# Interleaving the projection blocks of a two-layer encoder group by group, and taking weight scaling, rotation products and norm chains off two engines

## The chip, the cores and the metric

The kernel runs on one core of a Trainium2 chip. A core has five engines with queues of their own: TensorE (PE in the profile, with its weight loads as PEld), VectorE (DVE), ScalarE (ACT), GpSimd (POOL) and SyncE (SP), which issues the DMA transfers here. The metric is the device time of one execution in microseconds (us). Before the change it was 2788.43 us, the median of 3 runs (2785.87 to 2791.42).

## What is computed

The input x has 2048 positions of 1024 channels. Each of two layers computes

```python
h = rmsnorm(x, pre_g[l])
proj = jnp.einsum('bsd,de->bse', h, w_in[l])
u_a, v_a, g_a, q, k, v, g_b = jnp.split(proj, idx, axis=-1)
y_a = gmlp_group(u_a, v_a, ln_a_g[l], ln_a_b[l], spatial_w[l], spatial_b[l]) * jax.nn.silu(g_a)
y_b = gqa_axial_attention(q, k, v, q_norm_g[l], k_norm_g[l], tables) * jax.nn.silu(g_b)
y = jnp.concatenate([y_a, y_b], axis=-1)
x = x + rmsnorm(jnp.einsum('bse,ed->bsd', y, w_out[l]), post_g[l])
```

The projection has 2816 columns: u, v and g of the gating part (512 each), q (512: 8 heads of 64), k and v (128 each) and g_b (512). Gating layer-normalises v, mixes it over positions inside chunks of 128 (`W_s v + b`) and multiplies it by u and silu(g). Attention has 8 query heads on 2 key heads, with a root-mean-square norm and an axial rotation on every q and k head.

## The kernel before, in words

**Precision.** A product is made in three passes. Each operand is split into a high part and a low part, and high x high, high x low and low x high are summed in PSUM (`PASSES`). So a block of 256 columns for 128 positions takes 3 x 8 = 24 products.

**Two phases a layer.** `Project.run` makes the projection, `attend` the attention and the output product. The change touches the first. Positions are worked on in 4 groups of 512, each of 4 tiles of 128. `hT_jobs` loads a tile of x (L330), squares it on ACT for the norm (L334), computes the reciprocal root with 8 one-column operations on DVE (`rsqrt_row_steps`, L135 to L139), scales the tile on DVE (L339), transposes it on PE, and leaves a high part (ACT, L349) and a low part (DVE, L350) in `hT`. In the second layer the tiles of groups 0 and 1 arrive already scaled from the end of the layer before. The x rows live in a pool of 5 buffers.

**Weights.** A block of 256 columns is loaded (L262). `split_w` multiplies it by the norm weight `g_col` in two halves on GpSimd (L277), takes the largest magnitude on DVE (L280), spreads it over partitions by a product (tile `pe`), derives a power of two, and writes the high part on ACT (L294) and the low part on DVE (L295), each in two halves of 1024 elements.

**Blocks of a layer, in PE's order before.** (1) For each group: the k and v block, then q block 0; (2) q block 1 for all groups; (3) the v block of gating for all groups, 48 products a tile; (4) g_b blocks 0 and 1, each for all groups; (5) four gate blocks of 128 g and 128 u columns, each for all groups, 48 products of 512 columns. What follows a block on the other engines differs widely. A q block goes through `norm_rope`: squares on ACT (L390) and sums on DVE (L391), a reciprocal root in 10 operations (L123 to L127), the scaling (L398), the product with the cosines on GpSimd (L400), four products with the sines on DVE (L403) and the sum (L405), for two banks; later a transposition and a low part (L451). A k block does the same at half the width, plus L436. A g_b block takes one tanh on ACT and one DVE operation a bank (L515, L516). The rotation table is loaded per group and multiplied by the gain on GpSimd (L382).

**Background jobs.** `Background` holds small jobs with due times in ticks. `proj_tok` ticks once every 8 products of 256 columns, `proj_ch` once every 4 products of 512, and a tick runs up to two due jobs. Transpositions of the next group, second halves of `split_w` (`rest`), the mixing of v (L488) and the row maxima of the scores for the first 8 attention units (`max_step`: one product of 512 columns into `pmax` and one reduction on DVE, L748, per tick, 128 of them a layer) run this way. `last_jobs` enters the maxima; before the change it is called between steps (3) and (4).

**What fixes the order.** PE's order is that of the program (`Pinned`). The queues of DVE, ACT, GpSimd and SP are ordered by a scheduler when the kernel is built; each engine then works its queue strictly in that order. PSUM has 7 banks for all these tiles.

Of the kernel before, what the change touches and what calls it, by code (L numbers as in the profile page):

```python
# [9 lines left out]
F32 = mybir.dt.float32  # L10
F32R = mybir.dt.float32r
# [28 lines left out]
def encoder(ctx: ExitStack, tc, x, w_in, w_out, pre_g, post_g, ln_a_g, ln_a_b,  # L40
# [100 lines left out]

    def rsqrt(ms, n, tag):
        y, steps = rsqrt_steps(ms, n, tag, nc.vector)
        for f in steps:
            f()
        return y
# [30 lines left out]
    class Project:  # L177
# [88 lines left out]
        def split_w(self, raw, delay, vec=False):  # L266
# [3 lines left out]
            col = small.tile([P, 16], F32, name="w_col", bufs=5)  # L270
            top, sq, inv = col[:, 0:2], col[:, 2:4], col[:, 4:5]
            w.e, w.u, w.hu, w.hu2, w.eps = [col[:, 8 + i:9 + i] for i in range(5)]
            for i in range(2):
                sl = slice(i * ND // 2, (i + 1) * ND // 2)
                engine = nc.vector if vec and i == 0 else nc.gpsimd
                g = self.g_col[:, sl].unsqueeze(2).broadcast_to([P, ND // 2, WB])
                engine.tensor_tensor(raw[:, sl], raw[:, sl], g, ALU.mult)  # L277
            for i in range(2):
                sl = slice(i * ND // 2, (i + 1) * ND // 2)
                nc.vector.tensor_reduce(top[:, i:i + 1], raw[:, sl].rearrange("p d e -> p (d e)"), AX.X, ALU.max,  # L280
                                        apply_absolute_value=True)
            nc.vector.tensor_tensor(sq, top, top, ALU.mult)

            def rest():
                ps = ps_t("pe")
                for i in range(2):
                    PE.matmul(ps[:, 0:1], spread_w, sq[:, i:i + 1], start=(i == 0), stop=(i == 1))
# [4 lines left out]
                for i in range(2):  # L292
                    sl = slice(i * ND // 2, (i + 1) * ND // 2)
                    nc.scalar.activation(w.hl[:, 0, sl], raw[:, sl], AF.Copy, scale=w.e)  # L294
                    nc.vector.scalar_tensor_tensor(w.hl[:, 1, sl].rearrange("p d e -> p (d e)"),  # L295
                                                   raw[:, sl].rearrange("p d e -> p (d e)"), w.e,
                                                   w.hl[:, 0, sl].rearrange("p d e -> p (d e)"),
                                                   ALU.mult, ALU.subtract)
# [14 lines left out]
        def hT_jobs(self, g, tail=False):  # L313

            hT = big_t([P, 2, ND, GRP], "hT", F16)
            xs = [None] * TPG
            act, dve = (ACT, DVE) if tail else (nc.scalar, nc.vector)

            def prep(j):
                def f():  # L320
                    done = self.l > 0 and g < HN
                    src = h_d[g * TPG + j] if done else x_src(self.l, g * TPG + j)
                    if done:
                        xs[j] = xt = [f_t("x_h") for _ in range(2)]
                        for i in range(2):
                            nc.sync.dma_start(xt[i], src[:, i * GRP:(i + 1) * GRP])
                        return
                    row = row_t("x_t")
                    xs[j] = xt = [row[:, 0:GRP], row[:, GRP:D]]
                    nc.sync.dma_start(row, src)  # L330
                    junk = ps_t("sq")
                    parts = small.tile([P, 2], F32, name="ss_x", bufs=4)
                    for i in range(2):
                        nc.scalar.activation(junk, xt[i], AF.Square, accum_out=parts[:, i:i + 1])  # L334
                    z = small.tile([P, 1], F32, name="rs_x", bufs=4)
                    for f in rsqrt_row_steps(parts, z, "x", nc.vector):
                        f()
                    for i in range(2):
                        nc.vector.tensor_scalar(xt[i], xt[i], z, None, ALU.mult)  # L339
                return f  # L340
# [44 lines left out]
        def norm_rope(self, banks, n, tb, eps):  # L385
# [10 lines left out]
            for i, src in enumerate(banks):  # L396
# [3 lines left out]
                nc.gpsimd.tensor_tensor(t1, qn, tbi[:, :, 0:1, :].broadcast_to([P, 2, n, HD]), ALU.mult)  # L400
# [58 lines left out]
        def do_va(self, g, vs, ws):  # L459
# [8 lines left out]
            for j, vh in enumerate(vs):  # L468
# [9 lines left out]
                def mix(c, s=s, j=j):  # L478
# [12 lines left out]
                    if c == 3:  # L491
                        nc.sync.dma_start(z_d[g][:, :, j * P:(j + 1) * P], s.zt)
                bg.add(1 + 5 * j, split)
# [3 lines left out]
        def do_gate(self, g, c, pg, pu, w):  # L497
            z = f_t("fb")
# [65 lines left out]
        def run(self, kv, first, last_jobs, first_wo):  # L564
# [23 lines left out]
            w_kv = self.w_kv  # L588
            raw = self.load_w([C_Q])
            if self.l == 0:  # L590
                w = []
                bg.add(8, lambda: w.append(self.split_w(raw, None, True)))
            else:
                w = [self.split_w(raw, 6)]
            for i, g in enumerate(gs):
                if i == 0:
                    for f in self.stores:
                        f()
                    self.stores = []
                if i + 1 < NG:  # L600
                    start(g + 1)
                if i == 1:
                    raw = self.load_w([C_Q + WB])
                self.do_kv(g, self.banked(hTs[g], w_kv), w_kv)
                if i == 2:
                    w_next = self.split_w(raw, W_DELAY)
                    raw = self.load_w([C_VA])
                assert w and w[0].ready
                self.do_q(g, self.banked(hTs[g], w[0]), 0, w[0])
                if i + 1 < NG:  # L610
                    while left[g + 1]:
                        left[g + 1].pop(0)()
                if i == 1:
                    self.spatial_weights()
            w = w_next
            assert w.ready
            for i, g in enumerate(gs):
                if i == 0:
                    va = [self.split_w(raw, W_DELAY)]
                    raw = self.load_w([C_VA + WB])  # L620
                if i == 2:
                    va.append(self.split_w(raw, W_DELAY))
                    raw = self.load_w([C_GB])
                self.do_q(g, self.banked(hTs[g], w), 1, w)
            ws = [row_t("ws", dt=F32R) for _ in range(2)]
            for i in range(2):
                nc.sync.dma_start(ws[i].bitcast(F32), ws_d[:, i])
            assert va[1].ready
            for i, g in enumerate(gs):
                vs = []  # L630
                for j in range(TPG):
                    ps = self.proj_tok(hTs[g], j, va[0])
                    self.proj_tok(hTs[g], j, va[1], ps, WB)
                    v = f_t("fv")
                    for b in range(2):
                        sl = slice(b * WB, (b + 1) * WB)
                        nc.scalar.activation(v[:, sl], ps[:, sl], AF.Copy, scale=va[b].u)
                    vs.append(v)
                if i == 2:
                    w = self.split_w(raw, W_DELAY)  # L640
                    raw = self.load_w([C_GB + WB])
                self.do_va(g, vs, ws)
            nc.gpsimd.memset(self.kv[1][HD:HD + 2], 1.0)
            self.scale_v()
            last_jobs()
            blocks = [[C_GA + c * P, C_U + c * P] for c in range(4)]
            gbs = []
            for b in range(2):
                assert w.ready
                gbs.append(w)  # L650
                for i, g in enumerate(gs):
                    self.do_gb(g, self.banked(hTs[g], w), b, w)
                    if i == 1:
                        w_next = self.split_w(raw, W_DELAY)
                        raw = self.load_w(blocks.pop(0))
                w = w_next
            assert self.scaled
            for b in range(2):
                nc.vector.tensor_scalar(self.two_g[:, b], self.two, gbs[b].e, NORM_SCALE, ALU.mult, ALU.mult)
            for c in range(4):  # L660
                assert w.ready
                for i, g in enumerate(gs):
                    pg = self.proj_ch(hTs[g], w, 0)
                    pu = self.proj_ch(hTs[g], w, P)
                    self.do_gate(g, c, pg, pu, w)
                    if i == 1 and c < 3:
                        w_next = self.split_w(raw, W_DELAY)
                        raw = self.load_w(blocks.pop(0)) if blocks else None
                    if c == 3:
                        hTs[g] = None  # L670
                        if i == 1:
                            first_wo()
                w = w_next
# [620 lines left out]
```

## Time and profile before

| what | value |
|---|---|
| the profiled execution's own time | 2788.67 us |
| its span | 2786.9 us |
| median of 3 runs | 2788.43 us |
| PE busy | 2626.5 us (94% of the span) |
| DVE busy | 1891.0 us (68%) |
| ACT busy | 1500.0 us (54%) |
| POOL busy | 1361.8 us (49%) |
| first score product, layer 0 | 637.2 us from the span's start |
| first score product, layer 1 | 2015.3 us from the span's start |

The profile is of one execution. "Busy" is the time in which an engine had at least one instruction under way; PE's products are pipelined, so a busy PE need not be at its peak. The two projections take the stretches from the start to 637 us and from 1404 to 2015 us; attention takes the rest.

### The profile page before, as it was taken

What the parts mean: (1) busy time and instruction counts of PE and PEld (TensorE: products, weight loads), DVE (VectorE), ACT (ScalarE), POOL (GpSimd) and SP (SyncE); (2) the same over time, 40 slices, a digit from 0 to 9 for tenths busy, and PEclk for the clock granted to TensorE, in tenths of its full rate; (3) what the DMA queues carried; (4) which work ended last, traced back from release to release, by engine and by line L of the source; (5) the groups of instructions that cost most, each with busy time, mean ns of one, the idle gap of its engine ahead of it and who ended that gap; (6) DMA issues with size and microseconds to landing.
All of it is one profiled execution on the core that took longest, in us unless ns stands there. A gap on an engine that the chain in (4) does not pass through costs nothing. (4 is left out here: it accounts for less than half of the span.)

```text
span 2786.9 us, 48753 instructions
## 1 busy us (share of the span) xinstructions
PE 2626.5 (94%) x18318; PEld 1543.7 (55%) x18318; DVE 1891.0 (68%) x3978; ACT 1500.0 (54%) x3007; POOL 1361.8 (49%) x1121
## 2 busy tenths in 40 slices
PE   5788999999999999999978889999999999999997
PEld 4677976444444444444557778864444444444444
DVE  7978797435665766666498878983366656566664
ACT  3432211127887777877644222111288877777774
POOL 2233210116786776776642322001187767677764
PEclk9899999999999999999999999999999999999999
DMA  4232132332222222222533221323232212221313
GB/s 155 67 118 63 54 94 67 89 86 85 85 68 79 78 90 82 89 89 73 171 133 99 82 63 54 95 70 95 83 90 72 84 60 79 76 81 48 111 38 137
DMA packets 245329, 239.13 MB, mean 86 GB/s; under 512 B 20706, under 2 KB 204130, under 8 KB 245092
## 3 DMA queue, kind: packets, MB, share of 16 engines
q1 hardware_dynamic: 245092, 236.01, 27.4%
q8 instruction: 144, 2.36, 0.4%
q14 instruction: 93, 0.76, 0.1%
HBM read 150.88 MB, written 85.07 MB: 85 GB/s over the span
## 5 line engine op out<-in xcount | busy, mean ns | idle before, releaser
L84 POOL TENSOR_TENSOR p_parts<-p_f,p_parts 128x512 f16<-128x512 f32 x872 | 1033.3, 1204 | 395.4 <-ACT p_f L84 304.5
L84 ACT ACTIVATE p_parts<-sp 128x512 f16<-128x512 f32 x1024 | 627.0, 612 | 295.1 <-PE sp L84 288.0
L84 PE MATMUL pp<-w_hl,hT 128*128 128x256 f16 x5376 | 675.5, 279 | 9.9 <-DVE hT L350 5.8
L84 DVE TENSOR_REDUCE mx<-pmax 128x1 f32<-128x512 f32 x768 | 511.1, 680 | 233.4 <-PE pmax L84 231.2
L84 PE MATMUL pout<-wo,y_t 128*128 128x512 f32 x1488 | 655.4, 504 | 1.0 <-ACT p_f L84 0.7
L84 PE MATMUL po<-p_parts,v_st 128*32 128x512 f16 (+1 forms) x3072 | 637.2, 382 | 0.3 <-ACT p_parts L84 0.3
L84 ACT ACTIVATE p_f<-sp 128x512 f32<-128x512 f32 x1024 | 627.8, 613 | 0.1
L84 PEld LDWEIGHTS <-hT 128*128 128x128 f16 x5376 | 527.7, 100 | 105.7 <-issue 14.0
L84 PE MATMUL pmax<-k_t,q_m 128*128 128x512 f16 x1024 | 386.0, 379 | 13.9 <-DVE mx L84 7.2
L84 PE MATMUL sp<-q_st,k_t 128*128 128x512 f16 x1024 | 389.2, 380 | 4.8 <-ACT p_f L84 2.6
L84 PE MATMUL sp<-q,k_t 66*128 66x512 f16 x1024 | 390.1, 381 | 0.0
L84 PEld LDWEIGHTS <-v_st 128*32 128x32 f16 (+1 forms) x3072 | 193.2, 96 | 308.6 <-issue 251.3
L84 PEld LDWEIGHTS pout<-wo,y_t 128*128 128x128 f32 x1488 | 280.7, 190 | 134.0 <-issue 15.1
L84 PE MATMUL pp<-hT,w_hl 128*128 128x512 f16 x1536 | 344.4, 379 | 0.0
L84 PEld LDWEIGHTS <-k_t 128*128 128x128 f16 (+1 forms) x2048 | 191.5, 98 | 183.5 <-issue 70.1
L84 PEld LDWEIGHTS <-w_hl 128*128 128x128 f16 x1536 | 150.3, 98 | 179.0
L84 PE MATMUL sums<-p_parts,one_h 128*32 128x512 f16 x2048 | 241.8, 379 | 0.0
L277 POOL TENSOR_TENSOR w_raw<-w_raw,g_col 128x1024 f32<-128x1024 f32 x43 | 82.6, 1942 | 246.9 <-DMA w_raw<-in_w_in_dram 232.9
L748 DVE TENSOR_REDUCE mx<-pmax 128x1 f32<-128x512 f32 x256 | 169.7, 683 | 33.4 <-PE pmax L84 31.8
L508 POOL TENSOR_TENSOR fl<-fa,fh 128x512 fp32r<-128x512 f32 x32 | 41.1, 1284 | 293.8 <-ACT fh L507 291.1
L84 DVE TENSOR_TENSOR p_parts<-p_f,p_parts 128x512 f16<-128x512 f32 x152 | 130.3, 858 | 68.6 <-ACT p_f L84 59.3
L84 PEld LDWEIGHTS <-q_m 128*128 128x128 f16 x1024 | 100.9, 99 | 107.1 <-DMA q_m<-q_d 3.2
(173 smaller groups left out, 2469.4 us busy)
## 6 DMA issues: line engine op xcount, KB each, us to landing
y_t<-y_d SPq DMA_DIRECT2D x56, 512.0 KB
w_raw<-in_w_in_dram SPq DMA_DIRECT2D x14, 1024.0 KB
x_t<-in_x_dram SPq DMA_DIRECT2D x16, 512.0 KB
wo_raw<-in_w_out_dram SPq DMA_DIRECT2D x16, 512.0 KB
z_d<-fb SPq DMA_DIRECT2D x32, 256.0 KB
w_raw<-in_w_in_dram SPq DMA_DIRECT2D x16, 512.0 KB
q_m<-q_d SPq DMA_DIRECT2D x64, 128.0 KB
gb_d<-fa SPq DMA_DIRECT2D x32, 256.0 KB
```

The lines of the kernel that those rows point to most:

```text
L84: return tc.keep_in_program_order(call(*args, **kw))
L277: engine.tensor_tensor(raw[:, sl], raw[:, sl], g, ALU.mult)
L508: nc.gpsimd.tensor_tensor(lo, th, hi.bitcast(F32), ALU.subtract)
L748: dve.tensor_reduce(s.mx[:, j, c:c + 1], ps, AX.X, ALU.max)
```

## The change

It does four things.

1. The order of blocks becomes a list (`order`), with jobs hung on places in it (`before`). First, for each group, k and v with g_b block 0 (below: the k rounds); then for each group q block 0 with g_b block 1 (the q rounds); then the v block for each group, with gate block 0 of the first two groups in between; then q block 1 of each group with gate blocks 0 and 1 in between; then gate block 1, and gate blocks 2 and 3 alternating. `last_jobs` is called after q block 1 and gate block 0 of the first and third group, so the row maxima now run beside three of the four q blocks 1 and the gate blocks.
2. The norm weight is no longer multiplied into the weight block. The maxima are taken per row block of the raw weights (8 columns), multiplied by `g_col` there, and the scale of the two parts becomes `e * g_col`, one column for each of 8 pieces of 256 elements, on ACT and on DVE.
3. The product with the cosines moves from GpSimd to DVE. The rotation table's gain stays on GpSimd.
4. The x tiles of a group wait for one norm chain of 11 operations on 4 columns (`rsqrt_rows`) instead of one chain of 8 each, and are scaled on ACT instead of DVE. Group 0 of layer 0 keeps one chain a tile.

```diff
+    def rsqrt_rows(parts, v):
...
+        m, z, t = [small.tile([P, n], F32, name=f"rr_{i}", bufs=2) for i in range(3)]
+        v.scalar_tensor_tensor(m, parts[:, :, 0], D * EPS, parts[:, :, 1], ALU.add, ALU.add)
+        v.tensor_scalar(z.bitcast(I32), m.bitcast(I32), -0.5, RSQRT_MAGIC, ALU.mult, ALU.add)
+        for c in (-3.0, -12.0, -768.0):
+            v.tensor_tensor(t, z, z, ALU.mult)
+            v.tensor_tensor(t, t, m, ALU.mult)
+            v.scalar_tensor_tensor(z, t, c, z, ALU.add, ALU.mult)
...
-                engine = nc.vector if vec and i == 0 else nc.gpsimd
-                g = self.g_col[:, sl].unsqueeze(2).broadcast_to([P, ND // 2, WB])
-                engine.tensor_tensor(raw[:, sl], raw[:, sl], g, ALU.mult)
...
+                nc.vector.tensor_reduce(top[:, sl], raw[:, sl], AX.X, ALU.max, apply_absolute_value=True)
+            nc.vector.tensor_tensor(top, top, self.g_col, ALU.mult)
+            nc.vector.tensor_reduce(sq, top, AX.X, ALU.max, apply_absolute_value=True)
...
+                nc.vector.tensor_scalar(w.eg, self.g_col, w.e, None, ALU.mult)
+                for d in range(ND):
+                    nc.scalar.activation(w.hl[:, 0, d], raw[:, d], AF.Copy, scale=w.eg[:, d:d + 1])
+                    nc.vector.scalar_tensor_tensor(w.hl[:, 1, d], raw[:, d], w.eg[:, d:d + 1], w.hl[:, 0, d],
...
-                    for i in range(2):
-                        nc.vector.tensor_scalar(xt[i], xt[i], z, None, ALU.mult)
...
+                    elif j == TPG - 1:
+                        z = rsqrt_rows(parts, nc.vector)
+                        for n in range(TPG):
+                            for i in range(2):
+                                nc.scalar.activation(xs[n][i], xs[n][i], AF.Copy, scale=z[:, n:n + 1])
...
-                nc.gpsimd.tensor_tensor(t1, qn, tbi[:, :, 0:1, :].broadcast_to([P, 2, n, HD]), ALU.mult)
+                nc.vector.tensor_tensor(t1, qn, tbi[:, :, 0:1, :].broadcast_to([P, 2, n, HD]), ALU.mult)
...
+            for g in gs:
+                if g > 0:
+                    shift(*(("q0", "gb1"), ("gb1", "va0"), ("va0", "va1"))[g - 1])
+                    before(lambda g=g: finish_trans(g))
+                if g + 1 < NG:
+                    before(lambda g=g: start(g + 1))
+                order += [("kv", g), ("gb0", g)]
+            before(self.spatial_weights, self.scale_v)
+            for g in gs:
...
+                order += [("q0", g), ("gb1", g)]
+            before(load_ws, spread_two)
+            for g in gs:
...
+                order.append(("va", g))
+                if 1 <= g < 3:
+                    order.append(("g0", g - 1))
...
+            order += [("q1", 0), ("g0", 2)]
+            before(last_jobs)
+            order += [("q1", 1), ("g0", 3)]
+            shift("g2", "g3")
+            order += [("q1", 2), ("g1", 0), ("q1", 3)]
+            shift("g3", None)
+            order += [("g1", 1), ("g1", 2), ("g1", 3)]
+            for g in gs:
+                order += [("g2", g), ("g3", g)]
```

**GpSimd's queue, first layer.** From the first weight block to the second q block, before (L277 is the weight scaling, L400 the cosine product, L382 the table's gain):

```order
L277 TENSOR_TENSOR w_raw<-w_raw,g_col 128x1024 x3
L382 TENSOR_TENSOR fa<-fa,gain_k 128x512
L277 TENSOR_TENSOR w_raw<-w_raw,g_col 128x1024 x2
L643 MEMSET k_t 2x4096
L277 TENSOR_TENSOR w_raw<-w_raw,g_col 128x1024 x2
L400 TENSOR_TENSOR fc<-fc,fa 128x2x128 x2
L382 TENSOR_TENSOR fa<-fa,gain_q 128x512
L400 TENSOR_TENSOR fc<-fc,fa 128x512 x2
```

The same queue after the change, from the first k block to the v blocks (L394 is the table's gain, L252 and L488 low parts of the mixing matrix and of v):

```order
L394 TENSOR_TENSOR fa<-fa,gain_k 128x512
L700 MEMSET k_t 2x4096
L394 TENSOR_TENSOR fa<-fa,gain_k 128x512 x3
L394 TENSOR_TENSOR fa<-fa,gain_q 128x512
L252 TENSOR_TENSOR fl<-wsT,fh 128x512 x2
L394 TENSOR_TENSOR fa<-fa,gain_q 128x512 x3
L488 TENSOR_TENSOR fl<-fv,fh 128x512 x7
```

GpSimd keeps the table's gain and the low parts; the weight scaling and the cosine products are gone from its queue.

**DVE's queue inside a group, first layer.** Before, in a round of k with q block 0, the rotation of q stands between the norm chains (L135 to L139) and scalings (L339) of the next group's x tiles:

```order
L398 TENSOR_TENSOR fc<-pp,rs_y 128x512
L139 TENSOR_SCALAR rs_x<-rs_t,rs_x 128x1
L403 TENSOR_TENSOR fc<-fc,fa 128x8x16 x4
L398 TENSOR_TENSOR fc<-pp,rs_y 128x512
L405 TENSOR_TENSOR fc<-fc 128x512
L403 TENSOR_TENSOR fc<-fc,fa 128x8x16 x4
L339 TENSOR_SCALAR x_t<-x_t,rs_x 128x512
L405 TENSOR_TENSOR fc<-fc 128x512
L339 TENSOR_SCALAR x_t<-x_t,rs_x 128x512
L136 TENSOR_SCALAR rs_x<-rs_m 128x1
```

After, in the second k round, the rotation of k (half as wide; L410 scaling, L412 cosines, L415 sines, L417 sum) stands with the pieces of the next weight block (L302), and behind them come low parts of hT (L362) and the g_b operation (L530):

```order
L410 TENSOR_TENSOR fc<-pp,rs_y 128x2x128
L302 SCALAR_TENSOR_TENSOR w_hl<-w_raw,w_col,w_hl 128x256
L412 TENSOR_TENSOR fc<-fc,fa 128x2x128
L415 TENSOR_TENSOR fc<-fc,fa 128x2x2x16 x4
L410 TENSOR_TENSOR fc<-pp,rs_y 128x2x128
L417 TENSOR_TENSOR fc<-fc 128x2x128
L412 TENSOR_TENSOR fc<-fc,fa 128x2x128
L415 TENSOR_TENSOR fc<-fc,fa 128x2x2x16 x4
L302 SCALAR_TENSOR_TENSOR w_hl<-w_raw,w_col,w_hl 128x256
L417 TENSOR_TENSOR fc<-fc 128x2x128
L302 SCALAR_TENSOR_TENSOR w_hl<-w_raw,w_col,w_hl 128x256 x6
L362 TENSOR_TENSOR hT<-pt,hT 128x4x128 x4
```

The q rotation has left the rounds in which x is prepared, and no scaling of x stands in DVE's queue.

**DVE's queue where the row maxima run, first layer.** After the change the reductions (L792, before L748) stand between the steps of a q block 1 and the gate operations (L516, L517):

```order
L410 TENSOR_TENSOR fc<-pp,rs_y 128x512
L792 TENSOR_REDUCE mx<-pmax 128x1
L412 TENSOR_TENSOR fc<-fc,fa 128x512
L415 TENSOR_TENSOR fc<-fc,fa 128x8x16 x4
L410 TENSOR_TENSOR fc<-pp,rs_y 128x512
L417 TENSOR_TENSOR fc<-fc 128x512
L412 TENSOR_TENSOR fc<-fc,fa 128x512
L415 TENSOR_TENSOR fc<-fc,fa 128x8x16 x4
L792 TENSOR_REDUCE mx<-pmax 128x1
L417 TENSOR_TENSOR fc<-fc 128x512
L792 TENSOR_REDUCE mx<-pmax 128x1 x2
L797 TENSOR_REDUCE m_neg<-mx 128x4
```

Before, the same reductions stood between the last steps of mixing (L488) and the g_b operations (L516):

```order
L748 TENSOR_REDUCE mx<-pmax 128x1 x3
L488 SCALAR_TENSOR_TENSOR fb<-pt,lng,zbias 64x128 x2
L748 TENSOR_REDUCE mx<-pmax 128x1
L516 SCALAR_TENSOR_TENSOR fa<-fa,pp 128x512
L488 SCALAR_TENSOR_TENSOR fb<-pt,lng,zbias 64x128 x2
L748 TENSOR_REDUCE mx<-pmax 128x1
```

The maxima have moved from beside light blocks to beside three heavy ones and the gate blocks.

More of the change, by code (lines that the diff above doesn't have):

```diff
@@ L316, in hT_jobs @@
             xs = [None] * TPG
+            single = self.l == 0 and g == 0
+            parts = small.tile([P, TPG, 2], F32, name="ss_x", bufs=2)
             act, dve = (ACT, DVE) if tail else (nc.scalar, nc.vector)
@@ L590, in run @@
+            load("gb0")
             if self.l == 0:
-                w = []
-                bg.add(8, lambda: w.append(self.split_w(raw, None, True)))
-            else:
[L594 to L614, printed above, removed]
@@ L628, in run @@
[L628 to L642, printed above, removed]
@@ L657, in run @@
[L657 to L673, printed above, removed]
+                bg.add(8, lambda: split("gb0"))
+            else:
+                split("gb0", 6)
@@ new lines, in run, with before, shift, spread_two @@
+            order, todo = [], {}
+            def before(*fs):
+                todo.setdefault(len(order), []).extend(fs)
+            def shift(name, nxt):
+                before(lambda: split(name, W_DELAY))
+                if nxt:
+                    before(lambda: load(nxt))
+            def spread_two():
+                assert self.scaled
+                for b in range(2):
+                    nc.vector.tensor_scalar(self.two_g[:, b], self.two, w[f"gb{b}"].e, NORM_SCALE, ALU.mult, ALU.mult)
@@ new lines, in finish_trans, with stores, load_ws @@
+            def finish_trans(g):
+                while left[g]:
+                    left[g].pop(0)()
+            def stores():
+                for f in self.stores:
+                    f()
+                self.stores = []
+            ws = []
+            def load_ws():
+                ws.extend(row_t("ws", dt=F32R) for _ in range(2))
+                for i in range(2):
+                    nc.sync.dma_start(ws[i].bitcast(F32), ws_d[:, i])
+            before(stores, lambda: load("q0"))
@@ new lines, in run @@
+            order += [("q1", 2), ("g1", 0), ("q1", 3)]
[3 more added lines that the diff above has]
+                order += [("g2", g), ("g3", g)]
+            for n, (name, g) in enumerate(order):
+                for f in todo.get(n, []):
+                    f()
+                block(name, g)
+                if name == "g3":
+                    hTs[g] = None
+                    if g == 1:
+                        first_wo()
```

111 lines of the change are left out of this document (60 added, 51 removed).

## Prediction

> **What bounds the kernel now.** I read the slices of the page first, then a table of windows over the two projections, then who PE waits for there, then the groups of DVE instructions of the stage that waits.
>
> ```profile
> PE   5788999999999999999978889999999999999997
> DVE  7978797435665766666498878983366656566664
> ```
>
> A slice is about 70 us. PE is below nine tenths only in slices 1 to 4 and 21 to 24, the heads of the two projections, and there DVE is at its fullest. In the windows, each engine's busy time and instructions stand behind the length, PEclk is the granted clock:
>
> ```profile
> 26.00:174.00 148.00, 121.07 (x956) 101.59 (x955) 131.85 (x387) 62.56 (x153) 39.48 (x27) 0.90 0.35 110
> 174.00:280.00 106.00, 90.31 (x761) 77.94 (x759) 89.52 (x223) 25.07 (x49) 35.19 (x24) 0.92 0.24 64
> 280.00:637.00 357.00, 355.44 (x2357) 233.09 (x2356) 232.46 (x487) 68.12 (x113) 51.17 (x36) 1.00 0.27 78
> 1404.00:1550.00 146.00, 113.00 (x920) 95.42 (x919) 130.44 (x346) 54.44 (x128) 48.33 (x38) 0.91 0.36 116
> 1550.00:1640.00 90.00, 74.79 (x614) 63.76 (x613) 77.46 (x187) 20.00 (x37) 31.44 (x21) 0.92 0.23 65
> 1640.00:2015.00 375.00, 372.90 (x2516) 248.81 (x2514) 243.85 (x519) 73.17 (x124) 55.12 (x39) 1.00 0.27 77
> ```
>
> From 280 and from 1640 us on PE is full at full clock and DVE has a third of its time free (232 of 357 us). Ahead of that PE waits and its clock is 0.90 to 0.92. What is a product worth at full clock? Three rows of PE's timeline, start and length first:
>
> ```profile
> 1789.75 1.04 PE L84 MATMUL pp<-w_hl,hT 128*128 128x256 f16 x8
> 1790.62 0.38 PE L84 MATMUL pmax<-k_t,q_m 128*128 128x512 f16 x1
> 1790.84 1.04 PE L84 MATMUL pp<-w_hl,hT 128*128 128x256 f16 x8
> ```
>
> Start to start, 8 products of 256 columns take 0.87 us (0.109 each) and one of 512 takes 0.22. Taking 0.109 for every PE instruction of the heads (projections and transpositions), layer 0 needs (956 + 761) x 0.109 = 187 us of its 254, layer 1 (920 + 614) x 0.109 = 167 us of its 236. So 67 and 69 us are lost, 136 in all, and that is the most that a better order can return, besides the start. Whom PE waits for, in 26 to 280 us (total, times, longest):
>
> ```profile
> PE pt L84 <- DVE k_t L436: 14.0, 2, 8.0
> PE pt L84 <- DVE fc L405: 8.1, 6, 3.8
> PE pt L84 <- DVE x_t L339: 6.2, 3, 3.6
> ```
>
> All are DVE. In 1404 to 1640 us one wait is as long as several of these, and it is not a matter of load but of order:
>
> ```profile
> PE pe L84 <- DVE w_col L282: 14.0, 1, 14.0
> ```
>
> What fills DVE in 26 to 280 us of layer 0 (busy, then mean ns, then idle time before):
>
> ```profile
> L403 DVE TENSOR_TENSOR fc<-fc,fa 128x128 f32<-128x128 f32 x64 | 37.5, 644 | 9.4 <-POOL fa L382 9.3
> L339 DVE TENSOR_SCALAR x_t<-x_t,rs_x 128x512 f32<-128x512 f32 x30 | 21.5, 751 | 0.0
> L350 DVE TENSOR_TENSOR hT<-pt,hT 128x512 f16<-128x512 f32 x32 | 21.5, 680 | 1.7 <-ACT hT L349 1.7
> L280 DVE TENSOR_REDUCE w_col<-w_raw 128x1 f32<-128x1024 f32 x12 | 14.4, 1208 | 2.1 <-POOL w_raw L277 2.1
> L405 DVE TENSOR_TENSOR fc<-fc 128x512 f32<-128x512 f32 x16 | 12.0, 751 | 0.0
> L398 DVE TENSOR_TENSOR fc<-pp,rs_y 128x512 f32<-128x512 f32 x16 | 10.9, 682 | 0.1
> L451 DVE TENSOR_TENSOR fl<-pt,fh 128x512 f16<-128x512 f32 x16 | 10.6, 680 | 4.2 <-ACT fh L450 4.2
> L138 DVE TENSOR_SCALAR rs_t<-rs_x,rs_m 128x1 f32<-128x1 f32 x42 | 10.5, 267 | 0.2
> L391 DVE TENSOR_REDUCE ms_q<-fb 128x8 f32<-128x512 f32 x16 | 10.3, 675 | 1.5 <-ACT fb L390 1.5
> L295 DVE SCALAR_TENSOR_TENSOR w_hl<-w_raw,w_col,w_hl 128x1024 f16<-128x1024 f32 x8 | 10.1, 1276 | 0.7 <-ACT w_hl L294 0.7
> L403 DVE TENSOR_TENSOR fc<-fc,fa 128x64 f32<-128x64 f32 x32 | 9.3, 350 | 0.0
> L139 DVE TENSOR_SCALAR rs_x<-rs_t,rs_x 128x1 f32<-128x1 f32 x43 | 8.1, 206 | 0.2
> L436 DVE TENSOR_TENSOR k_t<-pt,k_t 64x256 f16<-64x256 f32 x16 | 6.5, 406 | 0.8 <-ACT k_t L435 0.8
> ...
> L398 DVE TENSOR_TENSOR fc<-pp,rs_y 128x256 f32<-128x256 f32 x8 | 3.3, 416 | 0.1
> L405 DVE TENSOR_TENSOR fc<-fc 128x256 f32<-128x256 f32 x8 | 3.3, 413 | 0.1
> ```
>
> Rotation of q and k, scaling of x, the low parts of hT and the norm chains lead. Two of these prices are inflated. The lines of L403 and L339 by their durations (ns, least, median, greatest), then the worst place of L403 on DVE and what GpSimd did there:
>
> ```profile
> L403 DVE TENSOR_TENSOR fc<-fc,fa x96: 210/279/1975, 71.7 to 260.3; 128x128 f32<-128x128 f32 x64, 128x64 f32<-128x64 f32 x32
> L339 DVE TENSOR_SCALAR x_t<-x_t,rs_x x32: 469/478/3810, 23.5 to 128.9; 128x512 f32<-128x512 f32 x32
> 206.72 5.36 DVE L403 TENSOR_TENSOR fc<-fc,fa 128x128 f32<-128x128 f32 x4
> 207.89 3.83 POOL L277 TENSOR_TENSOR w_raw<-w_raw,g_col 128x1024 f32<-128x1024 f32 x2
> ```
>
> DVE's four operations end at 212.08, just behind GpSimd's at 211.72: DVE stood still while GpSimd worked. The Trainium skill (SBUF — State Buffer, Who interferes with whom) says why: an operation with two inputs in SBUF shares a read port with GpSimd, and the later one blocks for the whole instruction; these rows agree.
>
> **The change part by part.** *Start.* The first block no longer waits for GpSimd:
>
> ```profile
> 6.99 3.74 POOL L277 TENSOR_TENSOR w_raw<-w_raw,g_col 128x1024 f32<-128x1024 f32 x2 [5.67 <-DMA g_col<-in_pre_g_dram]
> ```
>
> Maxima run on the raw weights, so up to 3.7 us go, and the later waits for gains and x rows may hide a part. I take 3.
>
> *k rounds (k, v and g_b block 0).* Two rows more, from 300 to 480 us the operation of a g_b bank, and from the first 480 us a 512-element operation of ACT:
>
> ```profile
> L516 DVE SCALAR_TENSOR_TENSOR fa<-fa,pp 128x512 f32<-128x512 f32 x16 | 10.8, 676 | 0.2
> L334 ACT ACTIVATE sq<-x_t 128x512 f32<-128x512 f32 x27 | 16.2, 599 | 4.2 <-DVE rs_t L138 4.1
> ```
>
> PE per round: 192 products, 32 transpositions of x, 8 of k, so 236 x 0.109 = 25.7 us with the pe product. DVE per round, in durations: low parts of hT 8 x 0.68 = 5.4; k: sums 2 x 0.41, chain and mean square 11 x 0.2 = 2.2, scaling 2 x 0.42, cosines 2 x 0.41 (nearest row: L405 at that width), sines 8 x 0.35 = 2.8, sum 2 x 0.41, together 8.3; L436 4 x 0.41 = 1.6; g_b 2 x 0.68; one weight block: two maxima 2.4, eight pieces of 256, which show in no row and are priced by L405's 0.413, 3.3 (against 2 x 1.28 before, so 0.7 more), a dozen small ones 2; the common chain 11 x 0.2 = 2.2. The sum is 26.6 us, about PE's. Now a round costs 148 / 4 = 37 us with q block 0 in it. Between 26 and 37 I take 30, nearer the floor, since 12 us of rotation, 6 of scaling x and four chains are gone. So 4.5 us are lost in each of three rounds that prepare x, and 5 more in the first, where the x rows of group 1 still arrive through few buffers.
>
> The x scaling goes to ACT: 8 x 0.6 = 4.8 us a round, on an engine that was busy 62.56 of 148 us. Operation by operation it is dearer there, 0.478 us (L339's median) against 0.6; left on DVE it would make a k round 26.6 + 8 x 0.478 = 30.4 us of DVE work. The sum goes by the load: DVE is what PE waits for. The Trainium skill (ScalarE: Activation LUTs, Rules for kernel authors) says that multiplications belong on VectorE and not on ScalarE. The prices of the two rows agree with it; what it would make of the time is a rival below.
>
> *q rounds (q block 0 and g_b block 1).* PE: 192 + 16 transpositions, 22.7 us. A q block costs DVE, from the rows of 16 (two a block): 2 x (0.75 + 0.68 + 0.68 + 0.68) = 5.6, sines 8 x 0.644 = 5.2, chain 2.2, so 13.0 now. Without GpSimd's product beside it the sines cost between 0.21 and 0.644; at the median 0.279 they save 2.9, and the cosines add 2 x 0.75 = 1.5. So 11.6 with g_b 13, and half a weight block 3.9: 17 of 22.7. PE bounds; I count 1 us a round for both this and the v stage, 5 us a layer in all. At 0.644 it would be 19.9, still hidden, so the doubt costs nothing here.
>
> *v rounds with gate blocks.* The gate block's z is read back from memory shortly after the mixing that writes it; DVE has the mixing there, but PE has 48 products a tile. In the 5 us above.
>
> *q block 1 beside row maxima.* The maxima cost as now, shown by the 128 of layer 0, whose rows up to 480 us are
>
> ```profile
> L748 DVE TENSOR_REDUCE mx<-pmax 128x1 f32<-128x512 f32 x108 | 71.2, 682 | 11.5 <-PE pmax L84 10.8
> ```
>
> A block has 12 ticks. PE: 12 x (0.87 + 0.22) + 16 x 0.109 = 14.8 us for a q block, 13.1 for a gate block. DVE: 12 x 0.68 = 8.2, so 19.8 and about 10.3. A pair is 30.1 against 27.9, three pairs a layer, and two weight blocks of 7.7 fall in. The pairs lose 7 us; the rest finds room in the gate blocks behind. I take 8 a layer. Without the relief at L403 it would be 2.9 more in each of three blocks, 17 a layer.
>
> *Layer 1's start.* The wait of 14 us remains nearly whole: the reductions of g_b block 0 stand in DVE's queue behind the same last steps of the layer before. GpSimd's scaling no longer stands between; I count 2 us for it, 12 stay.
>
> *Sum.* Layer 0: 67 + 3 - (13.5 + 5) - 5 - 8 = 38.5. Layer 1 has two rounds with norms (9) and two with transpositions only (3 each): 69 - 12 - 15 - 5 - 8 = 29. Together 67.5 us off the profiled execution's 2788.67, that is 2721 us. The median of three, 2788.43, is the same to 0.01%. Attention is untouched.
>
> **The rivals.** *DVE stays the bound of the k rounds.* 26.6 us of DVE work in a fixed order, with ACT in the loop, leaves no room: rounds of 36 instead of 30 in seven rounds that carry transpositions or norms cost 40, so 2761. For it: the sums are equal; against it: DVE worked 89% of 26 to 174 us, so its queue can be kept full. *Hardly any loss is left.* Neighbouring DVE records overlap, so 26.6 is high; with rounds at PE's floor and no loss beside the maxima, 13 us come back in layer 0 and 9 + 8 in layer 1: about 2690. *ACT's scalings are late.* The 4.8 us stand in ACT's queue ahead of evacuations of the next banks; if nothing hides them in the five rounds with norms (three in layer 0, two in layer 1), 24 us come on top: 2745. For it: the 0.6 against 0.478; against it: ACT had over half its time free. This is the rule of the Trainium skill's ScalarE page as a mechanism of this kernel.
>
> *Slower: the common chain holds PE up.* No tile can be transposed before all four rows have come and been squared, 11 chain operations and the scalings are through, some 5 + 2 + 5 = 12 us in series. It falls on five rounds in the two layers; from 67.5 / 5 = 13.5 us a round it eats the whole gain, and at 20 the result is 2821. Against it: rows are loaded one round ahead, and transpositions begin 9 ticks (about 10 us) into a round. *The change does not act:* DVE's waits give way to others of the same size, 2788; against it is PE's fixed order.
>
> **How the numbers follow.** Forecast 48%, ACT late 6%, DVE still the bound 20%, hardly any loss 14%, slower 8%, no change 4%. About 0.2% (5.6 us) is what a measurement can tell from no change. Faster is 48 + 6 + 20 + 14 = 88%. The range runs from 2687, just below the second rival, to 2768, above the first with the 17 for 8 of the maxima in part; outside stay the slow case, no change and some 7% of tails.
>
> **What would show it.** In the profile after: L403's successor near 0.28 us instead of 0.644; DVE's share lower in the head and higher in the middle; rounds of about 30 us in the k stage; PE at full clock through the q and v rounds; short PE waits at pmax beside q block 1; the wait at pe in layer 1 near 12 us; the first scores near 599 and 66 us earlier than 2015. It is wrong if PE waits for ACT's scaled x tiles or loaded weights, or if the k rounds stay near 37 us.

## The result, and the profile after

The changed kernel takes 2750.72 us (median of 4 runs, 2749.42 to 2754.92), the kernel before, beside it, 2789.8. The ratio is 0.9865, 95% interval 0.9847 to 0.9882: faster by 1.2 to 1.5%, 39 us. The forecast was a gain of 67.5 us, to 2721 us. The time lies inside the range (2687 to 2768), but little more than half of the gain came.

The slices of the page after:

```profile
PE   5999988999999999999979999889999999999997
DVE  6677668846665766666488766788366666666664
```

Slices 2 to 4 and 22 to 24, the heads of the projections, have filled up; slices 1 and 21, with the starts of the two layers, have not. New dips of PE stand in slices 6 and 7 and in 26 and 27, and DVE is now at its fullest in 7 and 8, 21 and 22, and 27 and 28. The windows show the same; first the four k rounds of layer 0, each from its first product to that of the next (192 products of the two blocks a round):

```profile
23.59:63.81 40.22, 31.78 (x250) 27.33 (x251) 30.43 (x103) 29.97 (x71) 4.78 (x2) 0.87 0.44 141
63.81:91.64 27.83, 26.01 (x236) 23.28 (x234) 18.15 (x69) 23.29 (x59) 1.27 (x1) 1.00 0.42 134
91.64:118.16 26.52, 25.84 (x234) 23.26 (x234) 20.75 (x73) 19.98 (x48) 1.27 (x1) 1.00 0.24 71
118.16:145.80 27.64, 23.86 (x205) 20.74 (x202) 15.10 (x48) 6.55 (x17) 1.27 (x1) 0.94 0.28 79
```

then, in both layers, the last of the mixing of v, the stage of the row maxima, and for layer 0 what follows. The first product into `pmax` starts at 407.0 us, in layer 1 at 1767.6:

```profile
372.00:404.00 32.00, 26.92 (x156) 18.45 (x156) 25.30 (x66) 5.00 (x9) 8.76 (x6) 0.89 0.18 51
404.00:520.00 116.00, 100.25 (x573) 58.58 (x574) 94.49 (x221) 18.98 (x40) 7.60 (x6) 0.91 0.24 67
520.00:622.00 102.00, 102.00 (x477) 46.34 (x475) 56.92 (x92) 16.86 (x30) 11.66 (x9) 1.00 0.27 81
1730.00:1764.00 34.00, 29.12 (x177) 20.45 (x175) 27.55 (x82) 5.23 (x9) 8.49 (x6) 0.90 0.14 36
1764.00:1870.00 106.00, 92.70 (x544) 55.64 (x545) 89.84 (x209) 17.25 (x38) 7.88 (x7) 0.92 0.23 70
```

From 404 to 520 us PE is idle for 116 - 100.25 = 15.8 us, and at a clock of 0.91 the busy rest does, by this estimate, 100.25 x 0.09 = 9 us less: 25 us lost. The same sum gives 8 us for 372 to 404, ahead of the first maximum, so 33 us in all. In layer 1 it is 21 and 8. Before the change the same stretch of layer 0 was full:

```profile
372.00:520.00 148.00, 147.75 (x1016) 99.57 (x1015) 122.10 (x224) 23.49 (x37) 16.33 (x11) 1.00 0.30 86
```

In the changed kernel DVE is busy 94.5 us from 404 to 520, beside 100.25 x 0.91 = 91 us of PE's work at full clock. By the amount of work alone some 3 us would be lost there (an estimate), not 25.

The stages in us, from the traces: layer 0 up to its first score product, and layer 1 from the last output product of layer 0 to its own first score. The last two columns give the time of the whole and its ratio to before.

| kernel | layer 0 | layer 1 | median | ratio (95%) |
|---|---|---|---|---|
| before | 637.2 | 618.3 | 2789.8 | 1 |
| changed | 622.2 | 592.8 | 2750.7 | 0.9865 (0.9847 to 0.9882) |
| order alone | 646.5 | 613.9 | 2793.8 | 1.0013 (1.0003 to 1.0023) |
| parts 2 to 4 alone | 611.9 | 594.8 | 2741.4 | 0.9831 (0.9816 to 0.9845) |
| weights alone | 622.5 | 603.6 | 2761.1 | 0.9896 (0.9882 to 0.9911) |
| weights and cosines alone | 614.0 | 595.2 | 2747.2 | 0.9851 (0.9835 to 0.9868) |
| changed, weights on GpSimd | 641.0 | 609.3 | 2786.2 | 0.9992 (0.9982 to 1.0002) |
| changed, cosines on GpSimd | 631.6 | 599.3 | 2765.5 | 0.9920 (0.9903 to 0.9937) |
| changed, x scaled on DVE | 615.1 | 589.5 | 2745.0 | 0.9844 (0.9829 to 0.9858) |
| changed, a chain per tile | 616.8 | 589.3 | 2743.7 | 0.9837 (0.9822 to 0.9853) |
| changed, gain early | 618.1 | 592.0 | 2746.4 | 0.9846 (0.9831 to 0.9861) |
| changed, maxima late | 607.9 | 580.5 | 2723.7 | 0.9765 (0.9751 to 0.9780) |
| late, gain early, chain per tile | 603.7 | 580.6 | 2716.3 | 0.9739 (0.9724 to 0.9753) |
| the same, x on DVE too | 603.6 | 580.0 | 2718.6 | 0.9741 (0.9727 to 0.9756) |

Layer 0 gave 15.0 us where 38.5 were forecast, layer 1 25.5 where 29 were. The attention stages, which no kernel touches, scatter by some 3 us (759.8 before, 763.5 after in layer 0; 754.3 and 756.8 in layer 1) and take 6 us of the gain of the profiled executions back. The profiled execution of the changed kernel is the longest of its four (2754.92 us), so its stages show 34 of the 39 us.

### The profile page after: what moved, and what is told of

It reads as the page before. It is cut to its first block, busy times and chain, and to the rows that moved or that the text cites. A ratio compares the mean times of both kernels' runs of the same rounds, so it can differ in the third digit from the quotient of the medians.

```text
span 2753.1 us, 48684 instructions
## 1 busy us (share of the span) xinstructions
PE 2618.1 (95%) x18274; PEld 1539.0 (56%) x18274; DVE 1826.5 (66%) x4070; ACT 1549.9 (56%) x3187; POOL 1221.1 (44%) x1030
## 5 line engine op out<-in xcount | busy, mean ns | idle before, releaser
L84 PE MATMUL pp<-w_hl,hT 128*128 128x256 f16 x5376 | 644.4, 276 | 3.1 <-DVE hT L362 1.4
L84 PE MATMUL pp<-hT,w_hl 128*128 128x512 f16 x1536 | 378.9, 386 | 3.9 <-DVE fc L410 3.9
L792 DVE TENSOR_REDUCE mx<-pmax 128x1 f32<-128x512 f32 x256 | 171.7, 683 | 45.5 <-PE pmax L84 45.2
L488 POOL TENSOR_TENSOR fl<-fv,fh 128x512 fp32r<-128x512 f32 x32 | 43.7, 1385 | 240.1 <-ACT fh L487 221.1
```

The costliest lines, as they stand in the source:

```text
L84: return tc.keep_in_program_order(call(*args, **kw))
L488: nc.gpsimd.tensor_tensor(s.lo, vh, s.hi.bitcast(F32), ALU.subtract)
L792: dve.tensor_reduce(s.mx[:, j, c:c + 1], ps, AX.X, ALU.max)
```

## The experiments

**Row maxima late.** The theory after the result: what is lost comes from maxima that meet q block 1. They are entered behind the last q block 1 instead.

```diff
             order += [("q1", 0), ("g0", 2)]
-            before(last_jobs)
             order += [("q1", 1), ("g0", 3)]
             shift("g2", "g3")
-            order += [("q1", 2), ("g1", 0), ("q1", 3)]
+            order += [("q1", 2), ("q1", 3)]
+            before(last_jobs)
+            order += [("g1", 0)]
```

> The changed kernel with the row maxima entered behind the last q block 1, so that they run beside gate blocks only. Theory A: what is left of the loss (about 27 us of PE from 372 to 520 us in layer 0, 22 us from 1730 to 1860 us in layer 1) comes from maxima that meet the work of q block 1 and of its stores and weight blocks in the queues of DVE and SP. Then some 40 us return, less the waits at the mixing: 2710 to 2718 us, and PE is full from 410 us on in layer 0. Theory B: the 128 maxima cost DVE too much wherever they stand: the same waits at pmax come beside the gate blocks, 2740 to 2752 us.

2723.7 us: 27 us back, not 40, between the two theories. The waits of PE from 372 to 520 us (total, times, longest), in the changed kernel:

```profile
PE pmax L84 <- DVE mx L792: 8.9, 2, 4.5
PE pmax L84 <- DMA q_m<-q_d: 4.6, 1, 4.6
PE pt L84 <- DVE fb L500: 2.2, 1, 2.2
PE t L84 <- DVE m_neg L797: 1.9, 2, 1.2
PE pp L84 <- DVE fc L410: 1.9, 1, 1.9
```

and with the maxima late, where no wait for a reduction or for the load of `q_m` is left in this stretch, with windows of it:

```profile
PE pt L84 <- DVE fb L500: 2.2, 1, 2.2
PE pp L84 <- DVE fc L410: 1.8, 1, 1.8
PE pmax L84 <- DVE fc L410: 1.6, 1, 1.6
```

```profile
372.00:404.00 32.00, 27.62 (x165) 19.24 (x165) 25.57 (x67) 5.36 (x9) 8.34 (x6) 0.89 0.14 39
440.00:462.00 22.00, 17.68 (x86) 8.99 (x85) 20.92 (x57) 2.82 (x5) 0.00 (x0) 0.84 0.15 37
462.00:520.00 58.00, 58.00 (x278) 27.06 (x276) 49.17 (x93) 10.90 (x22) 5.39 (x5) 1.00 0.27 76
```

From 404 to 440 us PE is now full. Two losses of 7 us each remain. One lies in the mixing, from 372 to 404 us, and no place of the maxima touches it. The other lies from 440 to 462 us, where the first late maxima (from 446.9 us on) still meet the last rotation of q block 1. From 462 to 520 us PE issues a maximum about every 1.08 us beside gate blocks and does not wait once. So theory A holds for the maxima, and what it had put too low is the mixing.

**Order alone.** Weight scaling, cosines, chains and x scaling as before the change, in the new order.

```diff
-                    nc.scalar.activation(w.hl[:, 0, d], raw[:, d], AF.Copy, scale=w.eg[:, d:d + 1])
...
+                engine.tensor_tensor(raw[:, sl], raw[:, sl], g, ALU.mult)
...
-                nc.vector.tensor_tensor(t1, qn, tbi[:, :, 0:1, :].broadcast_to([P, 2, n, HD]), ALU.mult)
+                nc.gpsimd.tensor_tensor(t1, qn, tbi[:, :, 0:1, :].broadcast_to([P, 2, n, HD]), ALU.mult)
...
-                                nc.scalar.activation(xs[n][i], xs[n][i], AF.Copy, scale=z[:, n:n + 1])
...
+                        nc.vector.tensor_scalar(xt[i], xt[i], z, None, ALU.mult)
```

> Only the new order of blocks; weight scaling and cosine product on GpSimd, one norm chain a tile and scaling of x on DVE as before the change. Theory A: a k round has then 26.6 us of DVE work plus 3.8 of scaling and 5.4 of chains, about 35 us, and two-input operations stand still beside GpSimd again: five rounds lose 8 to 9 us each more, so 2785 to 2800 us, no gain over the kernel before. Theory B: the order alone does it, and the other three parts are worth nothing: 2748 to 2753 us.

2793.8 us, as theory A had it: no gain. Layer 0 is even longer than before, 646.5 for 637.2. Its second to fourth k round by the windows (the engines in the order PE, PEld, DVE, ACT, POOL):

```profile
69.54:99.12 29.58, 25.92 (x236) 23.50 (x236) 29.44 (x97) 18.16 (x44) 8.27 (x6) 0.98 0.38 126
99.12:127.50 28.38, 28.37 (x236) 24.88 (x236) 26.38 (x87) 13.76 (x32) 7.41 (x5) 0.90 0.23 66
127.50:158.60 31.10, 25.28 (x206) 21.69 (x204) 18.50 (x45) 7.44 (x15) 5.01 (x3) 0.89 0.25 70
```

The heads are not as bad as theory A had them (35 us a round): 29.6, 28.4, 31.1. From 372 to 560 us PE is busy 165.85 of 188 at 0.92, the loss in the mixing and beside the maxima again.

**Parts 2 to 4 alone**, in the order of before: the diffs of the change in the weights, the cosines and the norm, with no line of the order.

> The order of before with the three other parts (norm weight in the scale, cosines on DVE, common norm chain with the scaling on ACT). Theory A: a round of k with q block 0 falls from 37 us to about 33, four rounds in each layer, and the start gains 3: 2755 to 2765 us, with the maxima undisturbed where they stood. Theory B: without the order DVE stays as full in these rounds: 2780 to 2790 us.

2741.4 us, faster than either theory said, and faster than the whole change. The longest wait of its head in layer 0 is that for scaled x tiles:

```profile
PE pt L84 <- ACT x_t L339: 15.3, 3, 10.4
```

**Gain early.** A second buffer for the q gain of the next layer.

```diff
-            self.gain_q = lay.tile([P, 2, HD], F32, name="gain_q")
+            self.gain_q = lay.tile([P, 2, HD], F32, name="gain_q", bufs=2)
```

> The changed kernel with a second buffer for the q gain, so that layer 1's gain is loaded long before DVE reaches the operation that waits for it at 488 to 494 us of layer 0. Theory A: the 4.4 us of PE idle behind it and the lower clock that follows go: 2743 to 2747 us. Theory B: another wait takes its place within the same q block: 2749 to 2753 us.

In the changed kernel DVE came at 488 us to an operation on a gain whose load had just been queued, and stood 5.93 us in the middle of a reciprocal root; the maxima queued behind it held PE:

```profile
494.06 0.29 DVE L230 TENSOR_SCALAR gain_q<-gain_q,g_exp 128x128 f32<-128x128 f32 x1 [5.93 <-DMA gain_q<-in_q_norm_g_dram]
...
494.56 0.68 DVE L792 TENSOR_REDUCE mx<-pmax 128x1 f32<-128x512 f32 x1
495.16 0.16 DVE L125 TENSOR_TENSOR rs_t<-rs_y 128x16 f32<-128x16 f32 x1
```

2746.4 us: layer 0 ends 4.1 us sooner and layer 1 is as long, as theory A says. The intervals of the two kernels overlap, though every run of the one is below every run of the other.

**Weights on GpSimd again**, the rest as changed.

```diff
-                nc.vector.tensor_reduce(top[:, sl], raw[:, sl], AX.X, ALU.max, apply_absolute_value=True)
-            nc.vector.tensor_tensor(top, top, self.g_col, ALU.mult)
...
+                engine.tensor_tensor(raw[:, sl], raw[:, sl], g, ALU.mult)
```

> The changed kernel with the norm weight multiplied into the weight blocks on GpSimd again; order, cosines, chain and scaling of x as changed. Theory A: GpSimd's 3.8 us a block make DVE's two-input operations stand still, four blocks in each k and q stage, and the first block waits 3 us again: 2768 to 2785 us, the greatest of the three parts. Theory B: the k rounds have room for that now: 2751 to 2757 us.

2786.2 us, a microsecond above theory A's range: taking this one part back loses 35 us of the 39. The first k round takes 50.2 us for 40.2, the next two 30.2 and 28.1 for 27.8 and 26.5. The small chain operations show the stops: one line of DVE by its durations (least, median, greatest), with the weights on GpSimd and in the changed kernel:

```profile
L127 DVE SCALAR_TENSOR_TENSOR rs_y<-rs_t,rs_y x96: 150/167/1893, 58.3 to 1884.9; 128x16 f32<-128x16 f32 x48, 128x8 f32<-128x8 f32 x24, 128x4 f32<-128x4 f32 x24
```

```profile
L127 DVE SCALAR_TENSOR_TENSOR rs_y<-rs_t,rs_y x96: 151/166/177, 46.4 to 1851.9; 128x16 f32<-128x16 f32 x48, 128x8 f32<-128x8 f32 x24, 128x4 f32<-128x4 f32 x24
```

Six of the 96 operations took 1.18 to 1.89 us, and each ended within 0.05 us of a GpSimd instruction. The longest, with what GpSimd did then:

```profile
183.14 1.89 DVE L127 SCALAR_TENSOR_TENSOR rs_y<-rs_t,rs_y 128x16 f32<-128x16 f32 x1
178.75 6.25 POOL L289 TENSOR_TENSOR w_raw<-w_raw,g_col 128x1024 f32<-128x1024 f32 x2 [0.87 <-PE pt L84]
```

The operation ended at 185.03 us, GpSimd's two products at 185.00. GpSimd's durations and waiters in this kernel are

```profile
L289 POOL TENSOR_TENSOR w_raw<-w_raw,g_col x44: 1887/1893/4400, 7.0 to 1727.1; 128x1024 f32<-128x1024 f32 x44
...
  DVE w_col L292: 15.5, 7
```

The longest product, 4.40 us, is the second of the two above: two low parts of a weight block on DVE (L307, two inputs in SBUF, 1.27 us each) ran first, from 180.66 to 183.21 us; the rows read as GpSimd held up by DVE as well. The stops are only a part: seven times a maximum had to wait for the product, 15.5 us in all, and PE's wait at the start of layer 1 is 17.7 us for 12.5. How the 35 us divide among these was not separated.

**Cosines on GpSimd again.**

```diff
-                nc.vector.tensor_tensor(t1, qn, tbi[:, :, 0:1, :].broadcast_to([P, 2, n, HD]), ALU.mult)
+                nc.gpsimd.tensor_tensor(t1, qn, tbi[:, :, 0:1, :].broadcast_to([P, 2, n, HD]), ALU.mult)
```

> The changed kernel with the cosine product on GpSimd again. Theory A: the sines stand still beside it, about 2.9 us a q block less the 1.5 saved, hidden in the q rounds, not hidden in the three q blocks 1 beside the maxima and in the k rounds: 2755 to 2765 us. Theory B: hidden everywhere: 2748 to 2753 us.

2765.5 us, 15 us lost, at the upper end of theory A. The sines beside GpSimd, and in the changed kernel (columns as in the prediction's groups):

```profile
L415 DVE TENSOR_TENSOR fc<-fc,fa 128x128 f32<-128x128 f32 x64 | 31.8, 554 | 0.3
```

```profile
L415 DVE TENSOR_TENSOR fc<-fc,fa 128x128 f32<-128x128 f32 x64 | 14.2, 281 | 0.0
```

The q rounds of layer 0 hide it (23.4, 26.6, 22.0 and 21.8 us in both kernels). The time goes elsewhere, layer 0's k rounds with 5 us of the 9.4 among it; the rest was not separated.

**x scaled on DVE again, common chain kept.**

```diff
-                                nc.scalar.activation(xs[n][i], xs[n][i], AF.Copy, scale=z[:, n:n + 1])
+                                nc.vector.tensor_scalar(xs[n][i], xs[n][i], z[:, n:n + 1], None, ALU.mult)
```

> The changed kernel with the scaling of x on DVE again, common chain kept. Theory A: the k rounds run at PE's rate now (2 to 3 us lost in 40 from 60 us on) and take 3.8 us more of DVE a round without loss: 2747 to 2754 us. Theory B: DVE is still what ends a k round, five rounds by 3.8: 2766 to 2772 us.

2745.0 us, 5.8 us faster than the change and faster than either theory allowed. The intervals of the two ratios overlap slightly, but every run is below every run of the changed kernel. Its second and third k round run at PE's rate:

```profile
63.89:89.47 25.58, 25.58 (x236) 23.29 (x234) 21.25 (x77) 18.92 (x51) 1.27 (x1) 1.00 0.44 145
89.47:114.93 25.46, 25.46 (x235) 23.28 (x234) 24.70 (x83) 15.72 (x40) 1.27 (x1) 1.00 0.25 74
```

So ACT's scalings cost 1 to 2 us a k round: in the second, ACT, not DVE, was the fuller engine (23.29 of 27.8 us against 18.15). DVE's wait for ACT's evacuation of k shows it, in the second and third k round of the changed kernel and of this one:

```profile
DVE k_t L448 <- ACT k_t L447: 10.7, 2, 5.3
```

```profile
DVE k_t L448 <- ACT k_t L447: 0.6, 2, 0.4
```

The Trainium skill (ScalarE: Activation LUTs, Rules for kernel authors) has multiplications on VectorE: the run agrees, with 6 us instead of the rival's 24.

**A norm chain per tile again, scaling on ACT kept.**

```diff
-            single = self.l == 0 and g == 0
+            single = True
```

> The changed kernel with one norm chain a tile again, scaling on ACT kept. Theory A: the common chain costs PE only the wait of 6.8 us for the first scaled tile of group 1 in layer 0, and the chains of five rounds (5.4 us of DVE each) find room: 2741 to 2748 us, faster than the changed kernel. Theory B: five rounds lose 5.4 us each: 2770 to 2778 us.

2743.7 us, 7.0 faster than the change, as theory A said (here too the intervals overlap slightly and the runs do not). The changed kernel's wait in the first k round, from 26 to 130 us,

```profile
PE pt L84 <- ACT x_t L351: 6.8, 1, 6.8
```

shrinks to 2.8 us, and that round takes 36.6 us for 40.2. With x scaled on DVE and the common chain kept, a pause of 7.1 us stands at the same place, so it comes from the chain and not from ACT.

**All that helped, together.** Late maxima, early gain and a chain per tile; then with the scaling on DVE too, which leaves nothing of part 4. The diffs are those above.

> The changed kernel with three edits: row maxima behind the last q block 1, a second buffer for the q gain, one norm chain a tile (scaling stays on ACT). Theory A: the three waits lie in different places and their gains add up: 2723.7 from the late maxima, less 7 of the chain, less 0 to 4 of the gain: 2712 to 2717 us, faster than all kernels so far. Theory B: the gains cover each other: 2720 to 2725 us.

> As the one before, with the scaling of x back on DVE too, so that the whole fourth part of the change is undone. Theory A: the k rounds have room for 3.8 + 5.4 us more of DVE work, so that part 4 is worth nothing in the new order: 2712 to 2720 us. Theory B, which follows from the sum of 26.6 us of DVE work against 25.7 of PE in a k round: 36 us of DVE work then hold PE up in five rounds, by 5 to 9 us each: 2737 to 2760 us.

2716.3 and 2718.6 us, the fastest kernels here and the same within their intervals: theory A for both. With a chain per tile in place, moving the scaling as well gains nothing, so the 7 and the 6 us above do not add up. The second kernel has a DVE that is full in its second and third k round, and PE still runs at its rate:

```profile
65.40:91.22 25.82, 25.63 (x234) 23.29 (x234) 25.72 (x106) 19.39 (x52) 1.27 (x1) 1.00 0.44 148
91.22:117.03 25.81, 25.63 (x235) 23.29 (x235) 25.63 (x102) 15.73 (x40) 1.27 (x1) 1.00 0.24 72
```

The durations of DVE's records that start in the first of these windows sum to 34.0 us, near theory B's 36, but the records overlap and cover 25.9.

**Weights alone, and weights with cosines, in the order of before.** The diffs of the change for these parts (the first q block's half that DVE had scaled goes too).

> The kernel before with the norm weight in the scale of the parts and nothing else changed. Theory A: GpSimd's weight scaling is the greatest of the costs by itself, most of the 48 us that the three parts give without the order: 2750 to 2760 us. Theory B: as long as the cosine product stays on GpSimd, DVE's stops beside it remain and little is won: 2772 to 2786 us.

> The kernel before with the norm weight in the scale and the cosine product on DVE; chains and scaling of x as before. Theory A: the common chain with scaling on ACT costs as much as it saves here too (PE waits 15.3 us in layer 0 and 9.0 in layer 1 for tiles scaled on ACT): 2732 to 2744 us, no slower than the three parts together (2741.4). Theory B: 9 us of DVE work a round are needed in these full rounds: 2752 to 2770 us.

2761.1 and 2747.2 us. The weights alone give 29 us, a microsecond beyond theory A's range; x scaling on DVE falls to its undisturbed price (751 ns before),

```profile
L396 DVE TENSOR_TENSOR fc<-fc,fa 128x128 f32<-128x128 f32 x64 | 33.5, 582 | 8.4 <-POOL fa L375 8.3
...
L332 DVE TENSOR_SCALAR x_t<-x_t,rs_x 128x512 f32<-128x512 f32 x28 | 12.6, 479 | 0.0
```

while the sines (L396) stay at 582 until the cosines go too, for 14 us more. (An x scaling has one input in SBUF and a scalar per partition; before, it stopped too, up to 3.81 us beside GpSimd's clearing of `k_t`, L643.) The second lies between its theories: part 4 gives 6 us on top in this order (2741.4), with intervals that overlap.

## Why the prediction had the sign and missed the size

Taken stage by stage, with PE's idle time and its lower clock added up as above, the sum compares so (us of PE lost):

| stage | layer 0, priced | layer 0, measured | layer 1, priced | layer 1, measured |
|---|---|---|---|---|
| start of the layer | | | 12 | 12.5 |
| k rounds | 18.5 | 20 | 15 | 4 |
| q and v rounds, with the mixing | 5 | 9 | 5 | 8 |
| from the first maximum on | 8 | 25 | 8 | 21 |

That the time fell inside the range owes something to luck: in layer 1 the k rounds were priced 11 us too dear, which made up for most of what the maxima cost there (25.5 us came of 29), while layer 0 had no such balance (15.0 of 38.5).

*The start*: PE's first projection product comes at 23.6 us for 26.2; 3 was said. Right.

*The k rounds*: 40.2, 27.8, 26.5 and 27.6 us in layer 0; 39.9, with the wait at the layer's start in it, 26.8, 26.4 and 22.0 in layer 1. The two at 30 were priced too dear by 2 to 4 us, the first, at 35, too cheap by 5. The fourth prepares no x and had no loss in the sum, but a wait of 3.8 us stands in it: that of PE's product into `pe`, for the next weight block, which the profile puts down to DVE's low part of k (L448). The sum of 26.6 us of DVE work was too high, as the rival *hardly any loss* had it: in the second and third round the durations of DVE's records sum to 21.8 and 25.0 us, and by the windows DVE was busy 18.15 and 20.75. So a part was priced too dear, and a part is the overlap of neighbouring records, which mean durations times counts leave out. L403's successor at 0.281 us came as forecast. (The rival's own sum leaves out layer 0's 8 us beside the maxima; with them it comes to about 2683 us, below the range.)

*DVE stays the bound* fell. *ACT's scalings are late* was right in kind, at 6 us. *The common chain holds PE up* happened once, 7 us, not in five rounds of 13.5; it is also the one place where the prediction's own sign of being wrong, PE waiting for ACT's scaled x tiles, showed at length.

*The q rounds*: 23.4, 26.6, 22.0 and 21.8 us in layer 0, where 22.7 had been priced, and PE without a pause in them; the longest holds 16 products for the mixing weights as well. Right.

*v rounds*: PE runs without a pause until 371 us, and then the last mixing holds it up, 8 us in each layer, for which the 5 us of both stages had little room. Before the change the mixing cost PE next to nothing.

*Layer 1's start*: 12 us were to stay, and 12.5 did:

```profile
PE pe L84 <- DVE w_col L289: 12.5, 1, 12.5
```

*q block 1 beside row maxima* is the step that failed: "I take 8 a layer". The stretch lost 25 us in layer 0 and 21 in layer 1. The step compared sums over pairs of blocks, 30.1 us for 27.9, and let the rest "find room in the gate blocks". But each maximum is one product that PE issues in a fixed place and one reduction in DVE's strict queue, with PSUM banks between them for a few: what counts is the longest stretch without a reduction, not the mean. Between the reductions at 449.36 and 460.64 us DVE works 10.6 us without a pause on other things, the reciprocal root, the steps of two rotations and eight pieces of a weight block (L302); the end of it, and the wait of PE,

```profile
458.66 2.06 DVE L302 SCALAR_TENSOR_TENSOR w_hl<-w_raw,w_col,w_hl 128x256 f16<-128x256 f32 x5
460.64 0.68 DVE L792 TENSOR_REDUCE mx<-pmax 128x1 f32<-128x512 f32 x1
...
461.38 0.59 PE L84 MATMUL pmax<-k_t,q_m 128*128 128x512 f16 x1 [4.54 <-DVE mx L792]
```

A second such stretch is the load of the next layer's gain (its second buffer gave 4.1 us back), and a third wait is for the first load of `q_m`, which stood in SP's queue behind stores of gate results. Moving the maxima gave 14.3 and 12.3 us back, so that much of the 25 and 21 is shown to be theirs. Of the remainder, 7 us in layer 0 lie where the late maxima meet the last rotation; how the lower clock and the other waits share the rest was not separated. More PSUM banks for the maxima were not tried.

The change as made is therefore several things that work against each other: parts 2 and 3 give 43 us by themselves, and the new order, worth nothing alone, gives 29 more (2747.2 to 2718.6, both without part 4) once the maxima are kept off most of q block 1 and the gain comes early.

## What to carry to other kernels

Price a stage of two strict queues by its longest gap, not by its mean load: list what can stand between two consecutive items of the chain, the rare things too (a weight block, the next layer's constants). When an engine is relieved, look whose port and queue the old work held: here taking a scaling off GpSimd, which had time for it, gave 29 us through other engines. And try each part of a change alone: here the order by itself gave nothing, and in the new order taking back the common chain or the scaling on ACT gained 7 and 6 us.

## What the runs showed of the hardware

- A DVE operation with two inputs in SBUF can stop for a whole GpSimd instruction whatever its own size: 0.167 us became 1.893, so small operations can lose many times their own length. The Trainium skill (SBUF — State Buffer, Who interferes with whom) has the one who comes second wait for the whole instruction; these rows agree. It goes both ways: a GpSimd product of 1.89 us took 4.40 behind two such operations of DVE.
- The granted clock falls after a few microseconds of idle PE. In the changed kernel PE stood from 490.94 to 495.30 us; the rows below show the clock before, in and after this pause. At 0.50 four products of 512 columns take 1.91 us for 1.03. A pause of 2.24 us, to 390.55, was also followed by a lower clock (0.68 over 392 to 396 us), one of 1.19 us, to 432.74, was not (1.00 over 432 to 440). From 404 to 520 us this was about a third of the loss (9 of 25 us).

```profile
484.00:492.00 8.00, 6.94 (x33) 3.02 (x31) 4.03 (x11) 0.75 (x2) 1.26 (x1) 1.00 0.06 13
492.00:496.00 4.00, 0.70 (x2) 0.25 (x2) 1.84 (x8) 0.00 (x0) 0.00 (x0) 0.70 0.30 103
496.00:500.00 4.00, 4.00 (x11) 1.38 (x10) 4.00 (x10) 0.00 (x0) 0.00 (x0) 0.50 0.00 0
500.00:504.00 4.00, 3.36 (x15) 1.28 (x13) 4.00 (x12) 0.00 (x0) 0.00 (x0) 0.95 0.02 4
```

- DVE records overlap with their neighbours: a reduction of 0.68 us at 494.56 is followed by an operation at 495.16, 0.60 later; with small operations between large ones, records that sum to 34.0 us covered 25.9. The Trainium skill (Perfetto Trace Analysis, Optimizing Scalar/DVE Operations) says that the end of an operation, its write acknowledgement, overlaps with the next one; the rows agree.
